# A hybrid RWKV-7 / attention block: inverse square roots as one GpSimd power, RWKV outputs transposed in squares of 32, removal products on GpSimd

## The chip, the cores and the metric

The kernel runs on one core of one Trainium2 chip. The metric is the device time of one execution in microseconds (us); lower is better. Five engines work side by side, each through its own queue in order: TensorE (PE, matrix products), VectorE (DVE), ScalarE (ACT), GpSimd (POOL) and SyncE (SP, which issues most of the loads). An instruction that needs another engine's result waits on a semaphore at the head of its queue, and everything behind it waits too.

## The reference

One layer on 256 tokens of width 2048, in fp32. Only the RWKV branch is touched in substance:

```python
u = rms_norm(h); z = u @ w_in                       # split into RWKV, attention and gate columns
kk = heads(k * k_k)                                 # 16 heads of 64
kk = kk / jnp.maximum(jnp.sqrt(jnp.sum(kk * kk, axis=-1, keepdims=True)), 1e-12)
k = k * (1 + (a - 1) * k_a)
# scan over tokens; -kk and kk * a are the removal ("delta rule") vectors
sa = einsum(state, -kk_t);  state = state * w_t + sa * (kk_t * a_t) + v_t * k_t;  y_t = einsum(state, r_t)
y = (y - mean) * lax.rsqrt(var + 64e-5)             # per head
y = y * lnx_w + lnx_b
y_rw = (y + bonus) * g
mix = (sigmoid(gA) * (y_rw @ Wa) + sigmoid(gB) * (y_mla @ Wb)) @ W_out
h += rms_norm(mix); h += rms_norm(gated MLP(h)); h += rms_norm(sigmoid(h @ W_pg) * (p @ W_ple))
```

There are inverse square roots in every `rms_norm`, in the normalization of `kk` and in the per-head normalization of `y`.

## The kernel before

All weights stream from HBM in chunks of 128x1024 fp32 (`wchunk`, L135). Each half of 512 columns is split into a rounded part `hi` (ACT cast, L148) and a rest `lo` (DVE subtraction, L149), five buffers each, so that a product in fp32 is made of three faster ones: hi by hi, hi by rest, lo by hi. `dense` and `fm3` (L183 to L185) do that with weights stationary, `fm` (L170, L174) and `tm` (L196 to L200) for the later layers. So each 512 columns of weights cost one ACT and one DVE instruction, all through the program.

The RWKV heads go in eight pairs (128 partitions: two heads of 64), two pairs at a time, which makes four duos. `rw_pair` (L714) is a generator: each `yield` names how many units of dense work (one unit is six matmuls of 128x256) are emitted before its next step. A loop at the end advances up to three duos together: `cur` runs the state recurrence, `nxt` prepares the next duo's operands, `old` finishes the former duo's outputs, and between the steps `work` emits the dense matmuls of the input, gate and attention-output projections. So PE's queue is dense matmuls with the duo's small matmuls strewn in; the tile framework then places the instructions of each engine by priority and by its own estimates of when they can start. Which instruction stands where in a queue is fixed when the program is built.

What the change and the prediction's steps touch:

- `rsqrt` (L206): an inverse square root on DVE without a table. A first guess from the bit pattern (L208), a first correction (L212 to L214, or L210 and L214 where there is one column) and a second one (L218 to L222, or L216 to L222). That is nine small instructions for 2 or 4 columns, seven for one column. `rstd_col` (L224) scales a sum of squares (L227) and calls it: three times near the start, after w_out and w_down and in between (two columns), and in `finish` (L1326), once for each half of the tokens, at the end (one column).
- In `rw_pair`, preparation: squares of `kk` are summed by PE (`pq`, L768), clamped (L771) and rooted into `nv`; ACT spreads the root (`rb`, L775), PE transposes it (`nr`, L779), DVE multiplies (`kk`, L781). Then `kr` (L786, L787), the removal products `be` = kk times a (L790) and its scaled form in `bk` (L791), and `a` is overwritten in place (L792). POOL copies part of `bk` (L797). PE uses `bk` and `kr` in `pg` (L818).
- In `rw_pair`, recurrence: four chunks of `pc` products on PE (L940, L944, L953) with short ACT and DVE steps between them (`R` L942, `av` L946, `sv` L955). Each waits for the one before.
- In `rw_pair`, tail: mean and variance of `y` (L970 to L977), `rsqrt` into `gs`, the multiplication (L982); eight matmuls of 64x64 a pair against the identity transpose `y` into PSUM (`pm`, L988), ACT evacuates with scale and bias (`yf`, L990), DVE adds the bonus (L992), PE makes the gate `pgt` (L995 to L998), DVE multiplies (L999), and the result is split into `yrw` (L161, L162), which the branch product (L1087 on) reads.
- POOL otherwise does memsets and copies (`vw` L830/L831, `kb` L825, `Xb` L900, `av` L930) and later six additions (L1090).

Of the kernel before, what the change touches and what calls it, by code (L numbers as in the profile page):

```python
# [108 lines left out]
def hybrid_block(tc, A):  # L109
# [50 lines left out]
    def split(hi, lo, src):  # L160
        act(hi, src, AF.Copy)  # L161
        tt(out=lo, in0=src, in1=hi.bitcast(F32), op=ALU.subtract)  # L162
# [39 lines left out]


    RA, RB = 1.681914091, 0.703952253

    def rsqrt(dst, v, w):  # L206
        t, p = w
        ts(out=dst.bitcast(I32), in0=v.bitcast(I32), scalar1=-0.5, scalar2=float(0x5F1FFFF9), op0=ALU.mult, op1=ALU.add)  # L208
# [12 lines left out]
        tt(out=p, in0=p, in1=t, op=ALU.mult)
        stt(out=dst, in0=p, scalar=-1.875 * RB, in1=dst, op0=ALU.add, op1=ALU.mult)  # L222
# [491 lines left out]
    def rw_pair(J, j, k, r, v):  # L714
        par = j % 2

        def e1(nm, shape=None, dt=F32):
# [52 lines left out]
        nv = sp.tile([P, 4, 4], F32, name="nv")  # L770
        ts(out=nv[:, 0, :], in0=pq[:, 0:4], scalar1=1e-24, scalar2=None, op0=ALU.max)  # L771
# [3 lines left out]
        act(rb[:], nv[:, 1, :].unsqueeze(2).to_broadcast([P, 4, C]), AF.Copy)  # L775
# [14 lines left out]
        tt(out=be[:], in0=kk[:], in1=a[:], op=ALU.mult)  # L790
        tt(out=bk[:, :, 0:C], in0=c4(be[:]), in1=c4(pin[:]), op=ALU.mult)  # L791
# [176 lines left out]
        gs = sp.tile([P, 5, NCH], F32, name="gs")  # L968
# [14 lines left out]
        yield NONE, STEP
        yield NONE, STEP
        pm = small("pm")
        for c in range(NCH):
            for hs in (lo_, hi_):
                mm(pm[hs, c * C:c * C + C], y[hs, c, :], ident[hs, hs], start=c == 0, stop=c == NCH - 1)  # L988
# [1 line left out]
        act(y[:], pm[:, 0:T], AF.Identity, scale=V("lnx_w", j), bias=V("lnx_b", j))  # L990
# [1 line left out]
        tt(out=y[:], in0=y[:], in1=bo[:], op=ALU.add)  # L992
# [453 lines left out]
```

## Time and profile before

| quantity | value |
|---|---|
| time, median of 3 runs | 1560.78 us (1560.56 to 1561.42) |
| the profiled execution's own time | 1560.39 us |
| its span in the trace | 1558.6 us |
| busy, PE / DVE / ACT / POOL | 1538.0 / 1182.2 / 942.1 / 60.9 us |
| instructions in the trace, PE / DVE / ACT / POOL | 10850 / 2670 / 1944 / 125 |
| mean granted TensorE clock | 0.997 |
| RWKV duos | from 180 us to 586 us in the span |

A row of a group gives line, engine, operation, output and inputs by the program's names, shape, count, then busy time, mean duration in ns and the idle time of the engine just before them. A row of the timeline gives start, duration, engine, line, operation, and in brackets how long the engine had idled and what released it; instructions of the same line that follow each other are merged with their count. Matmuls overlap in PE's pipeline, so the distance from start to start is what one costs, not its duration. DVE's small instructions overlap in the same way by some tens of ns.

### The profile page before, as it was taken

The page shows a single profiled execution, that of the slowest core. Times are in us where ns is not written, and L with a number is a line of the kernel's source. Part 1 is how long each engine was busy: PE and PEld are TensorE (multiplying, and loading weights), DVE is VectorE, ACT ScalarE, POOL GpSimd, SP SyncE. Part 2 cuts the span into 40 slices and gives each one's busy share as a digit, 9 for nine tenths or more (in the row PEclk, how much of TensorE's full clock was granted, in tenths as well). Part 3 has the DMA queues.
Part 4 walks back from the last instruction along what each step waited for, and adds up shares of the span by engine and source line. Part 5 has one row for each costly group of instructions (what it writes and reads, how often), then busy time and mean ns, then how long its engine had stood idle before and what let it go on. Part 6 is the DMA issues. An engine that isn't in the chain of part 4 may idle for free.

```text
span 1558.6 us, 29636 instructions
## 1 busy us (share of the span) xinstructions
PE 1538.0 (99%) x10850; PEld 1388.3 (89%) x10850; DVE 1182.2 (76%) x2670; ACT 942.1 (60%) x1944; POOL 60.9 (4%) x125
## 2 busy tenths in 40 slices
PE   9999999999999999999999999999999999999997
PEld 9989999999999999887888888888888888888886
DVE  7896687898989776557787777777777655777866
ACT  7686756566565555456766555555655555776653
POOL 0000201101011102000000000000000000000000
PEclk9999999999999999999999999999999999999998
DMA  8654555454444546865656555565655666666564
GB/s 304 192 172 141 154 173 164 138 171 129 147 150 136 160 153 200 306 199 167 203 174 205 198 181 202 179 203 179 206 181 190 175 192 195 197 197 191 166 200 148
DMA packets 80482, 285.19 MB, mean 183 GB/s; under 512 B 9040, under 2 KB 10320, under 8 KB 80336
## 3 DMA queue, kind: packets, MB, share of 16 engines
q1 hardware_dynamic: 77760, 279.48, 56.3%
q10 hardware_dynamic: 2576, 3.81, 0.7%
q8 instruction: 85, 1.39, 0.4%
q14 instruction: 61, 0.50, 0.1%
HBM read 281.16 MB, written 2.10 MB: 182 GB/s over the span
## 4 chain that ended last, share of the span: by engine, by line
PE 89%; DVE 6%; ACT 2%; DMA 1%; issue 1%; DVEq 0%; ACTq 0%
PE d L170 21%; PE d L174 11%; PE d L183 9%; PE d L185 8%; PE d L184 8%; PE o L196 7%; PE o L198 6%; PE o L200 6%; PE e L196 2%; PE e L198 2%; PE e L200 2%; DVE lo L149 2%; ACT hi L148 1%; DMA raw<-in_w_in 1%; PE tr L237 0%
## 5 line engine op out<-in xcount | busy, mean ns | idle before, releaser
L149 DVE TENSOR_TENSOR lo<-raw,hi 128x512 fp32r<-128x512 f32 x684 | 461.0, 690 | 213.9 <-ACT hi L148 208.5
L148 ACT CAST hi<-raw 128x512 fp32r<-128x512 f32 x684 | 410.7, 619 | 297.9 <-PE o L200 97.9
L183 PE MATMUL d<-uT,hi 128*128 128x256 f32 x1072 | 307.7, 287 | 0.7 <-ACT hi L161 0.6
L170 PE MATMUL d<-u,highs 128*128 128x512 f32 x1312 | 305.5, 390 | 0.0
L185 PE MATMUL d<-uT,lo 128*128 128x256 f32 x1072 | 300.5, 280 | 0.7 <-DVE lo L162 0.2
L184 PE MATMUL d<-uT,hi 128*128 128x256 f32 x1072 | 299.6, 279 | 0.1
L170 PEld LDWEIGHTS d<-u,highs 128*128 128x128 f32 x1312 | 243.3, 188 | 48.9
L148 ACT CAST highs<-raw 128x512 fp32r<-128x512 f32 x328 | 186.8, 616 | 115.0 <-DMA raw<-in_w_up 80.3
L183 PEld LDWEIGHTS d<-uT,hi 128*128 128x128 f32 x1072 | 201.7, 188 | 2.8 <-ACT hi L161 0.8
L185 PEld LDWEIGHTS d<-uT,lo 128*128 128x128 f32 x1072 | 201.5, 188 | 2.1 <-DVE lo L149 1.1
L184 PEld LDWEIGHTS d<-uT,hi 128*128 128x128 f32 x1072 | 201.7, 188 | 0.4 <-DVE uT L290 0.3
L149 DVE TENSOR_TENSOR hi<-raw,highs 128x512 fp32r<-128x512 f32 x164 | 112.7, 688 | 76.8 <-PE d L174 58.8
L174 PE MATMUL d<-u,lo 128*128 128x256 f32 x752 | 117.7, 280 | 0.0
L149 DVE TENSOR_TENSOR lo<-raw,highs 128x512 fp32r<-128x512 f32 x164 | 112.0, 684 | 0.0
L174 PE MATMUL d<-u,hi 128*128 128x256 f32 x656 | 103.3, 279 | 0.0
L174 PEld LDWEIGHTS d<-u,lo 128*128 128x128 f32 x752 | 101.7, 188 | 0.8
L174 PEld LDWEIGHTS d<-u,hi 128*128 128x128 f32 x656 | 91.5, 188 | 3.5
L198 PE MATMUL o<-lo,fsplit 128*128 128x512 f32 x264 | 88.6, 389 | 0.0
L196 PE MATMUL o<-hi,fsplit 128*128 128x512 f32 x264 | 88.5, 389 | 0.0
L200 PE MATMUL o<-hi,fsplit 128*128 128x512 f32 x264 | 88.4, 389 | 0.0
L1228 ACT ACTIVATE cy<-d 128x512 f32<-128x512 f32 x44 | 26.2, 597 | 67.8 <-PE d L174 67.8
L198 PEld LDWEIGHTS o<-lo,fsplit 128*128 128x128 f32 x264 | 49.6, 188 | 10.7 <-DVE lo L149 0.3
(389 smaller groups left out, 2550.9 us busy)
## 6 DMA issues: line engine op xcount, KB each, us to landing
raw<-in_w_up SPq DMA_DIRECT2D x176, 512.0 KB, 4.3
raw<-in_w_in SPq DMA_DIRECT2D x133, 512.0 KB, 3.6
raw<-in_w_down SPq DMA_DIRECT2D x88, 512.0 KB, 4.3
raw<-in_w_out SPq DMA_DIRECT2D x32, 512.0 KB, 4.4
raw<-in_w_pg SPq DMA_DIRECT2D x32, 512.0 KB, 3.6
raw<-in_w_bm SPq DMA_DIRECT2D x16, 512.0 KB, 3.7
raw<-in_w_br SPq DMA_DIRECT2D x16, 512.0 KB, 3.7
raw<-in_w_kv SPq DMA_DIRECT2D x8, 512.0 KB, 3.6
```

What stands on the lines that cost most here:

```text
L148: nc.scalar.copy(hi[:], raw[:, c:c + 512])
L149: tt(out=lo[:], in0=raw[:, c:c + 512], in1=hi[:].bitcast(F32), op=ALU.subtract)
L170: mm(ps[:, c, :], hi(i, col, P), mov[i][2], start=first and x == 0 and i == 0, stop=False)
L174: mm(ps[:, c, 0:T], lo(i, col, P), mov[i][0], start=False, stop=last and x == len(parts) - 1 and i == len(mov) - 1)
L183: mm(ps[:, c, :], hi(i, col, P), mov[i][:, 0:T], start=f, stop=False)
L184: mm(ps[:, c, :], hi(i, col, P), mov[i][:, T:2 * T], start=False, stop=False)
L185: mm(ps[:, c, :], lo(i, col, P), mov[i][:, 0:T], start=False, stop=l)
L196: mm(b[:], h, hi(i, g * 512, 512), start=f, stop=False)
L198: mm(b[:], h, lo(i, g * 512, 512), start=False, stop=False)
L200: mm(b[:], x, hi(i, g * 512, 512), start=False, stop=l)
L1228: act(y[:], ps[:, :, 0:T], AF.Copy)
```

## The change

1. `rsqrt` becomes one GpSimd `tensor_tensor` with the operation `pow`; the exponent -0.5 stands in eight columns of `st`. The clamp or the scaling ahead of it stays on DVE. In `rw_pair` the two pairs of a duo share one tile, and the second pair's step takes both pairs' eight columns in one power.
2. The tail's transposition: DVE transposes `y` in squares of 32x32 (one instruction a pair), ACT copies all of it, and four GpSimd copies a pair move the squares off the diagonal, across quadrants of 32 partitions. The eight `pm` matmuls are gone. Scale and bias, which ACT did at the evacuation, move into two DVE instructions that replace the two of L992 and L999. The tail has one `yield` less.
3. The removal products `be` and the part of `bk` made from it go from DVE to GpSimd. The in-place update of `a` stays on DVE, after them.

```diff
--- before.py
+++ after.py
@@ -200,32 +200,16 @@
                     mm(b[:], x, hi(i, g * 512, 512), start=False, stop=l)
 
 
-
-    RA, RB = 1.681914091, 0.703952253
-
-    def rsqrt(dst, v, w):
-        t, p = w
-        ts(out=dst.bitcast(I32), in0=v.bitcast(I32), scalar1=-0.5, scalar2=float(0x5F1FFFF9), op0=ALU.mult, op1=ALU.add)
-        if dst.shape[1] == 1:
-            ts(out=t, in0=dst, scalar1=dst, scalar2=v, op0=ALU.mult, op1=ALU.mult)
-        else:
-            tt(out=t, in0=dst, in1=dst, op=ALU.mult)
-            tt(out=t, in0=t, in1=v, op=ALU.mult)
-        stt(out=dst, in0=t, scalar=-RA / RB, in1=dst, op0=ALU.add, op1=ALU.mult)
-        if dst.shape[1] == 1:
-            ts(out=t, in0=dst, scalar1=dst, scalar2=v, op0=ALU.mult, op1=ALU.mult)
-        else:
-            tt(out=t, in0=dst, in1=dst, op=ALU.mult)
-            tt(out=t, in0=t, in1=v, op=ALU.mult)
-        ts(out=p, in0=t, scalar1=-0.375 * RB ** 5, scalar2=1.25 * RB ** 3, op0=ALU.mult, op1=ALU.add)
-        tt(out=p, in0=p, in1=t, op=ALU.mult)
-        stt(out=dst, in0=p, scalar=-1.875 * RB, in1=dst, op0=ALU.add, op1=ALU.mult)
+    nc.gpsimd.memset(st[:, 48:56], -0.5)
+
+    def rsqrt(dst, v):
+        nc.gpsimd.tensor_tensor(out=dst, in0=v, in1=st[:, 48:48 + dst.shape[1]], op=ALU.pow)
 
     def rstd_col(dst, ss, n):
-        v = sp.tile([P, 6], F32, name="rv")
+        v = sp.tile([P, 2], F32, name="rv")
         w = dst.shape[1]
         ts(out=v[:, 0:w], in0=ss, scalar1=1.0 / n, scalar2=1e-6, op0=ALU.mult, op1=ALU.add)
-        rsqrt(dst, v[:, 0:w], (v[:, 2:2 + w], v[:, 4:4 + w]))
+        rsqrt(dst, v[:, 0:w])
 
 
     def to_fm(ptile, dst, rows, gain, kbs):
@@ -767,12 +751,17 @@
         for t in range(2):
             mm(pq[:, 2 * t:2 * t + 2], sq[:, t * P:t * P + P], K("hsel", 0, 2), start=t == 0, stop=t == 1)
         yield NONE, STEP
-        nv = sp.tile([P, 4, 4], F32, name="nv")
-        ts(out=nv[:, 0, :], in0=pq[:, 0:4], scalar1=1e-24, scalar2=None, op0=ALU.max)
-        rsqrt(nv[:, 1, :], nv[:, 0, :], (nv[:, 2, :], nv[:, 3, :]))
+
+        if par == 0:
+            J["nv"] = sp.tile([P, 2, 2, 4], F32, name="nv")
+        nv = J["nv"]
+        ts(out=nv[:, 0, par, :], in0=pq[:, 0:4], scalar1=1e-24, scalar2=None, op0=ALU.max)
+        if par == 1:
+            nvs = [nv[:, i].rearrange("p r n -> p (r n)") for i in range(2)]
+            rsqrt(nvs[1], nvs[0])
         yield NONE, STEP
         rb = e1("rb", [P, 4, C])
-        act(rb[:], nv[:, 1, :].unsqueeze(2).to_broadcast([P, 4, C]), AF.Copy)
+        act(rb[:], nv[:, 1, par, :].unsqueeze(2).to_broadcast([P, 4, C]), AF.Copy)
         yield NONE, STEP
         nr = small("nr")
         for t in range(2):
@@ -787,8 +776,8 @@
         tt(out=kr[:, :, C:P], in0=c4(r), in1=pp[:, :, 1:C + 1], op=ALU.mult)
         yield NONE, STEP
         be = e1("be")
-        tt(out=be[:], in0=kk[:], in1=a[:], op=ALU.mult)
-        tt(out=bk[:, :, 0:C], in0=c4(be[:]), in1=c4(pin[:]), op=ALU.mult)
+        nc.gpsimd.tensor_tensor(out=be[:], in0=kk[:], in1=a[:], op=ALU.mult)
+        nc.gpsimd.tensor_tensor(out=bk[:, :, 0:C], in0=c4(be[:]), in1=c4(pin[:]), op=ALU.mult)
         ts(out=a[:], in0=a[:], scalar1=V("k_a", j), scalar2=oka[:, j:j + 1], op0=ALU.mult, op1=ALU.add)
         yield NONE, STEP
         kp = e1("kp")
@@ -965,7 +954,9 @@
         act(y[:], cc(py), AF.Copy)
         yield TAIL, STEP
 
-        gs = sp.tile([P, 5, NCH], F32, name="gs")
+        if par == 0:
+            J["gs"] = sp.tile([P, 3, 2, NCH], F32, name="gs")
+        gs = J["gs"][:, :, par]
         bc4 = lambda ap: ap.unsqueeze(2).to_broadcast([P, NCH, C])
         nc.vector.tensor_reduce(out=gs[:, 0, :], in_=y[:], axis=AX.X, op=ALU.add)
         ts(out=gs[:, 0, :], in0=gs[:, 0, :], scalar1=1.0 / C, scalar2=None, op0=ALU.mult)
@@ -976,28 +967,32 @@
         nc.vector.tensor_reduce(out=gs[:, 1, :], in_=sq[:], axis=AX.X, op=ALU.add)
         ts(out=gs[:, 1, :], in0=gs[:, 1, :], scalar1=1.0 / C, scalar2=64e-5, op0=ALU.mult, op1=ALU.add)
         yield NONE, STEP
-        rsqrt(gs[:, 2, :], gs[:, 1, :], (gs[:, 3, :], gs[:, 4, :]))
-        for _ in range(3):
-            yield NONE, STEP
+        if par == 1:
+            g8 = [J["gs"][:, i].rearrange("p r n -> p (r n)") for i in range(3)]
+            rsqrt(g8[2], g8[1])
+        yield NONE, STEP
+        yield NONE, STEP
         tt(out=y[:], in0=y[:], in1=bc4(gs[:, 2, :]), op=ALU.mult)
-        yield NONE, STEP
-        yield NONE, STEP
-        pm = small("pm")
-        for c in range(NCH):
-            for hs in (lo_, hi_):
-                mm(pm[hs, c * C:c * C + C], y[hs, c, :], ident[hs, hs], start=c == 0, stop=c == NCH - 1)
-        y = e1("yf")
-        act(y[:], pm[:, 0:T], AF.Identity, scale=V("lnx_w", j), bias=V("lnx_b", j))
-        yield NONE, STEP
-        tt(out=y[:], in0=y[:], in1=bo[:], op=ALU.add)
+
+        yt = e1("yt", [P, NCH, 2, 32])
+        nc.vector.transpose(out=yt[:].rearrange("p c b n -> p (c b n)"), in_=y[:].rearrange("p c n -> p (c n)"))
+        yield NONE, STEP
+        y = e1("yf", [P, NCH, 2, 32])
+        act(y[:], yt[:], AF.Copy)
+        for i in range(4):
+            nc.gpsimd.tensor_copy(y[Q[i ^ 1], :, i % 2, :], yt[Q[i], :, 1 - i % 2, :])
+        yield NONE, STEP
+        yield NONE, STEP
+        y = y[:].rearrange("p c b n -> p (c b n)")
+        stt(out=y, in0=y, scalar=V("lnx_w", j), in1=bo[:], op0=ALU.mult, op1=ALU.add)
         yield NONE, STEP
         pg = small("pgt")
         mm(pg[:, 0:T], lgs[:, 0, :], LM[:, 3, :], start=True, stop=False)
         mm(pg[:, 0:T], lgs[:, 0, :], LM[:, 4, :], start=False, stop=False)
         mm(pg[:, 0:T], lgs[:, 2, :], LM[:, 3, :], start=False, stop=False)
         mm(pg[:, 0:T], lgs[0:96, 1, :], LM[0:96, 5, :], start=False, stop=True)
-        tt(out=y[:], in0=y[:], in1=pg[:, 0:T], op=ALU.mult)
-        split(yrw[:, j, 0:T], yrw[:, j, T:2 * T], y[:])
+        stt(out=y, in0=y, scalar=V("lnx_b", j), in1=pg[:, 0:T], op0=ALU.add, op1=ALU.mult)
+        split(yrw[:, j, 0:T], yrw[:, j, T:2 * T], y)
 
     def gate(i, tag="zt"):
```

How the queues change, at three places. In the rows, `lo<-raw,hi` is the weight split of L149, and the brackets name the engines whose semaphores the instruction waits for.

DVE where the second duo's preparation and the first duo's recurrence meet, before (`kk` normalized, then the removal products, the update of `a`, and the recurrence's `sv`):

```order
L781 TENSOR_TENSOR kk<-kk,nr 128x256 [waits PE_49] x2
L786 TENSOR_TENSOR kr_4252<-kk,pp_3889 128x4x64 [waits DVE_49]
L786 TENSOR_TENSOR kr_4256<-kk,pp_3894 128x4x64 [waits DVE_49]
L149 TENSOR_TENSOR lo<-raw,hi 128x512 [waits PE_49,Activation_49]
L946 TENSOR_SCALAR av<-pc 64x64 [waits Activation_49] x2
L790 TENSOR_TENSOR be<-kk,a 128x256 x2
L149 TENSOR_TENSOR lo<-raw,hi 128x512 [waits DMAHW3_49,PE_49,Activation_49]
L791 TENSOR_TENSOR bk_4251<-be,pin 128x4x64 [waits DVE_49]
L792 TENSOR_SCALAR a<-a,vec,oka 128x256
L955 SCALAR_TENSOR_TENSOR sv<-pc,pp_2647,s_4170 64x64 [waits PE_49]
```

The same place on DVE after the change:

```order
L770 TENSOR_TENSOR kk<-kk,nr 128x256 [waits PE_49] x2
L775 TENSOR_TENSOR kr_4193<-kk,pp_3848 128x4x64 [waits DVE_49]
L775 TENSOR_TENSOR kr_4197<-kk,pp_3853 128x4x64 [waits DVE_49]
L149 TENSOR_TENSOR lo<-raw,hi 128x512 [waits PE_49,Activation_49]
L935 TENSOR_SCALAR av<-pc 64x64 [waits Activation_49] x2
L781 TENSOR_SCALAR a<-a,vec,oka 128x256 [waits Pool_49] x2
L149 TENSOR_TENSOR lo<-raw,hi 128x512 [waits DMAHW3_49,PE_49,Activation_49]
L784 TENSOR_TENSOR kp<-z_2469,a 128x256 [waits DVE_49] x2
L944 SCALAR_TENSOR_TENSOR sv<-pc,pp_2624,s_4111 64x64 [waits PE_49]
```

The products are gone, and both updates of `a` stand together behind a wait for POOL, ahead of the recurrence's `sv`.

DVE in the first duo's tail, before (the end of both pairs' chains for the root, then the multiplication of `y` by it; `gm` belongs to the second duo):

```order
L220 TENSOR_SCALAR gs<-gs 128x4 [waits DVE_49]
L219 TENSOR_TENSOR gs<-gs 128x4 [waits DVE_49]
L221 TENSOR_TENSOR gs<-gs 128x4 [waits DVE_49]
L220 TENSOR_SCALAR gs<-gs 128x4 [waits DVE_49]
L222 SCALAR_TENSOR_TENSOR gs<-gs 128x4 [waits DVE_49]
L221 TENSOR_TENSOR gs<-gs 128x4 [waits DVE_49]
L821 TENSOR_TENSOR gm_4521<-pg_4571,cst 128x8x64 [waits PE_49]
L222 SCALAR_TENSOR_TENSOR gs<-gs 128x4 [waits DVE_49]
L821 TENSOR_TENSOR gm_4521<-pg_4572,cst 128x8x64 [waits PE_49]
L982 TENSOR_TENSOR y<-y,gs 128x256
L982 TENSOR_TENSOR y<-y,gs 128x256 [waits DVE_49]
```

The same place after the change:

```order
L968 TENSOR_SCALAR gs<-gs 128x4 [waits DVE_49]
L967 TENSOR_REDUCE gs<-sq_4457 128x4 [waits Activation_49]
L149 TENSOR_TENSOR lo<-raw,hi 128x512 [waits DMAHW1_49,PE_49,Activation_49]
L968 TENSOR_SCALAR gs<-gs 128x4 [waits DVE_49]
L975 TENSOR_TENSOR y<-y,gs 128x256 [waits Pool_49]
L975 TENSOR_TENSOR y<-y,gs 128x256
L149 TENSOR_TENSOR lo<-raw,hi 128x512 [waits PE_49,Activation_49]
L810 TENSOR_TENSOR gm_4461<-pg_4494,cst 128x8x64 [waits PE_49]
```

The chains are gone, eighteen small instructions for the two pairs, and the multiplication stands directly behind the last scaling (L968), with a wait for POOL.

POOL from the third duo's recurrence to the fourth duo's preparation, before:

```order
L930 COPY av<-sv 128x512 [waits Activation_49]
L797 COPY bk_7228<-bk_7228 64x4x64 [waits DVE_49,Pool_49]
L797 COPY bk_7232<-bk_7232 64x4x64 [waits DVE_49]
L830 MEMSET vw 64x4x64 [waits PE_49]
L831 COPY vw<-z_4933 64x4x64
```

The same place after the change:

```order
L919 COPY av<-sv 128x512 [waits Activation_49]
L206 TENSOR_TENSOR nv<-nv,st 128x8 [waits DVE_49]
L779 TENSOR_TENSOR be<-kk,a 128x256 [waits DVE_49]
L780 TENSOR_TENSOR bk_7085<-be,pin 128x4x64 [waits Pool_49]
L779 TENSOR_TENSOR be<-kk,a 128x256 [waits DVE_49]
L786 COPY bk_7085<-bk_7085 64x4x64 [waits Pool_49]
L780 TENSOR_TENSOR bk_7089<-be,pin 128x4x64 [waits Pool_49]
L786 COPY bk_7089<-bk_7089 64x4x64 [waits Pool_49]
L819 MEMSET vw 64x4x64 [waits PE_49]
```

The power and the four products have come in; the second pair's `be` stands behind the first pair's `be` and `bk`.

More of the change, by code (lines that the diff above doesn't have):

```diff
@@ L978, in rw_pair @@
         yield NONE, STEP
-        rsqrt(gs[:, 2, :], gs[:, 1, :], (gs[:, 3, :], gs[:, 4, :]))
-        for _ in range(3):
-            yield NONE, STEP
-        tt(out=y[:], in0=y[:], in1=bc4(gs[:, 2, :]), op=ALU.mult)
+        if par == 1:
+            g8 = [J["gs"][:, i].rearrange("p r n -> p (r n)") for i in range(3)]
+            rsqrt(g8[2], g8[1])
         yield NONE, STEP
         yield NONE, STEP
-        pm = small("pm")
-        for c in range(NCH):
-            for hs in (lo_, hi_):
-                mm(pm[hs, c * C:c * C + C], y[hs, c, :], ident[hs, hs], start=c == 0, stop=c == NCH - 1)
-        y = e1("yf")
-        act(y[:], pm[:, 0:T], AF.Identity, scale=V("lnx_w", j), bias=V("lnx_b", j))
-        yield NONE, STEP
-        tt(out=y[:], in0=y[:], in1=bo[:], op=ALU.add)
+        tt(out=y[:], in0=y[:], in1=bc4(gs[:, 2, :]), op=ALU.mult)
+        yt = e1("yt", [P, NCH, 2, 32])
+        nc.vector.transpose(out=yt[:].rearrange("p c b n -> p (c b n)"), in_=y[:].rearrange("p c n -> p (c n)"))
+        yield NONE, STEP
+        y = e1("yf", [P, NCH, 2, 32])
[6 more added lines that the diff above has]
+        stt(out=y, in0=y, scalar=V("lnx_w", j), in1=bo[:], op0=ALU.mult, op1=ALU.add)
         yield NONE, STEP
```

## The prediction

> **What bounds the kernel now.** I read the page first: the busy shares of the engines and the chain of work that ended last. Then a table by stage, PE's waits, and the timeline at the places where the change cuts.
>
> ```profile
> PE 1538.0 (99%) x10850; PEld 1388.3 (89%) x10850; DVE 1182.2 (76%) x2670; ACT 942.1 (60%) x1944; POOL 60.9 (4%) x125
> PE 89%; DVE 6%; ACT 2%; DMA 1%; issue 1%; DVEq 0%; ACTq 0%
> 240.00:515.00 275.00, 271.01 (x3014) 263.35 (x3013) 238.57 (x762) 164.02 (x383) 33.83 (x76) 1.00 0.48 146
> 1549.00:1558.60 9.60, 0.00 (x0) 0.00 (x0) 5.84 (x16) 0.88 (x3) 0.00 (x0) 0.59 0.49 182
> PE pc L940 <- DVE sv L955: 1.9, 4, 0.9
> PE px L882 <- DVE YH L893: 1.7, 4, 0.6
> PE tr L237 <- DVE u L241: 0.8, 2, 0.6
> ```
>
> PE sets the time: busy 99% of the span, and 89% of the last chain. The third row is the middle of the RWKV duos (the columns after the length are PE, PEld, DVE, ACT, POOL): of 275 us PE idles 4.0, while DVE is busy 87%, against 76% over the whole span. The three waits show what the idling is: PE stands for DVE in the recurrence, a few tenths at a time. So a matmul removed in this stage is worth nearly its whole issue distance, and DVE work removed there is worth at most a part of those 4.0 us. The fourth row is the end: PE has nothing left in the last 9.6 us, and what stands there in a chain counts in full. POOL is idle 96% of the time.
>
> **The `pm` matmuls go.** The group of all of them, one duo's as the timeline shows them, and the next dense matmul:
>
> ```profile
> L988 PE MATMUL pm<-cst,y 64*64 64x64 f32 x128 | 4.6, 221 | 0.0
> 316.98 1.15 PE L988 MATMUL pm<-cst,y 64*64 64x64 f32 x32
> 318.06 0.38 PE L183 MATMUL d<-uT,hi 128*128 128x256 f32 x1
> ```
>
> PE is occupied from 316.98 to 318.06, 1.08 us a duo, and 4 duos make **4.3 us** (the group's 4.6 counts the modelled ends). The matmuls around them are dense work that was ready, so that time comes back: -4.3. What replaces them lies on DVE, ACT and POOL, and its result is read by PE at the end of the stage only (below).
>
> **The roots leave DVE.** In `rw_pair` a root is nine instructions like the first row below, twice a pair; the other rows are what else DVE loses or gets.
>
> ```profile
> L222 DVE SCALAR_TENSOR_TENSOR gs<-gs 128x4 f32<-128x4 f32 x8 | 1.3, 158 | 0.0
> L790 DVE TENSOR_TENSOR be<-kk,a 128x256 f32<-128x256 f32 x8 | 3.0, 417 | 0.1
> L791 DVE TENSOR_TENSOR bk<-be,pin 128x256 f32<-128x256 f32 x8 | 3.4, 421 | 0.2
> L992 DVE TENSOR_TENSOR yf<-yf,bo 128x256 f32<-128x256 f32 x8 | 3.3, 417 | 0.3 <-ACT yf L990 0.3
> L888 DVE STREAM_TRANSPOSE YH<-Xc 128x128 f32<-128x128 f32 x8 | 2.2, 295 | 0.0
> L800 DVE SCALAR_TENSOR_TENSOR rk<-z,vec,kp 128x256 f32<-128x256 f32 x8 | 4.0, 494 | 0.0
> ```
>
> Removed: 16 x 9 x 0.158 = 22.8 us of roots and 8 x (0.417 + 0.421) = 6.7 us of products. Added: eight transposes of 256 columns, at most twice the 0.295 of 128, so 4.7 us, and 16 x (0.494 - 0.417) = 1.2 us because the two instructions behind them become three-operand ones like L800. Net DVE is relieved of about 23.6 us in a stage where PE's waits come from it. Bounds of what that is worth: nothing, if the recurrence's own latency makes the waits, and 2.5 us, if the waits for `sv` and `YH` fall by two thirds. I take **-1.0**, a quarter of the 4.0 idle, since the removed instructions stand beside only some of the waits.
>
> **What the power costs in `rw_pair`.** No row shows a power on POOL. The nearest ones:
>
> ```profile
> L754 POOL MEMSET pp<- 128x4 f32 x8 | 0.7, 112 | 0.3
> L1090 POOL TENSOR_TENSOR g<-g,mix 128x512 f32<-128x512 f32 x6 | 9.6, 1604 | 69.3 <-ACT hi L148 48.7 <-DVE g L1089 20.6
> 272.41 0.16 DVE L771 TENSOR_SCALAR nv<-pq 128x4 f32<-128x4 f32 x1 [0.96 <-PE pq L768]
> 273.82 0.16 DVE L771 TENSOR_SCALAR nv<-pq 128x4 f32<-128x4 f32 x1
> 277.62 0.42 ACT L775 ACTIVATE rb<-nv 128x256 f32<-128x256 f32 x1 [0.38 <-DVE nv L222]
> 279.71 0.60 PE L779 MATMUL nr<-cst,rb 128*128 128x128 f32 x4
> 308.58 0.16 DVE L977 TENSOR_SCALAR gs<-gs 128x4 f32<-128x4 f32 x1
> 311.42 0.15 DVE L222 SCALAR_TENSOR_TENSOR gs<-gs 128x4 f32<-128x4 f32 x1
> 284.90 0.42 DVE L791 TENSOR_TENSOR bk<-be,pin 128x256 f32<-128x256 f32 x1
> 285.45 0.46 POOL L797 COPY bk<-bk 64x256 f32<-64x256 f32 x1 [15.88 <-DVE bk L791]
> ```
>
> The lower end is a small POOL instruction without arithmetic, 0.11 us; the upper end 1.60, the dearest POOL instruction here, 512 columns of a product against the power's eight. I take 1.0: nine passes of the smallest kind, as many as the DVE chain had. [...]
>
> The way from DVE to POOL is 0.13 us (285.32 to 285.45). For `nv` both clamps are done at 273.98, the power at 275.1, where the chain ended near 277.6; PE reads the spread roots at 279.71, behind two ACT steps of 0.42. So the new chain has 278.87 - 274.11 = **4.8 us** before PE waits, and costs nothing at 1.0. For `gs` the scaling ends at 308.74 and the old chain at 311.57, 2.8 us; now DVE itself stands at the multiplication of `y` for 0.13 + 1.0, with the weight splits and the second duo's `gm` behind it, but in a place where 2.8 us of its own chain stood. No cost; the cover is the removed chain, and beyond it the five buffers of `lo`.
>
> **The removal products on POOL.** The added wait is DVE's: both `a` updates wait for the second `be`, which stands in POOL's queue behind the first pair's `be` and `bk`. Behind `a` stand a weight split, `kp` and the recurrence's `sv`, for which PE waits already.
>
> ```profile
> 281.17 0.75 DVE L781 TENSOR_TENSOR kk<-kk,nr 128x256 f32<-128x256 f32 x2
> 282.51 0.68 DVE L149 TENSOR_TENSOR lo<-raw,hi 128x512 fp32r<-128x512 f32 x1
> 285.24 0.41 DVE L792 TENSOR_SCALAR a<-a,vec,oka 128x256 f32<-128x256 f32 x1
> 286.58 0.90 DVE L955 SCALAR_TENSOR_TENSOR sv<-pc,pp,s 64x64 f32<-64x64 f32 x3
> 595.54 0.68 DVE L149 TENSOR_TENSOR lo<-raw,hi 128x512 fp32r<-128x512 f32 x1
> 595.70 1.68 POOL L1090 TENSOR_TENSOR g<-g,mix 128x512 f32<-128x512 f32 x1 [4.81 <-DVE g L1089]
> L797 POOL COPY bk<-bk 64x256 f32<-64x256 f32 x8 | 6.7, 840 | 70.1 <-DVE bk L791 70.1
> ```
>
> The first `kk` is there at 281.59, POOL starts at 281.72. Half of L1090's 1604 ns is 0.80 a product: three end at 284.1, two updates at 284.9, the split 285.6, both `kp` (0.75) 286.3, four `sv` (1.2) 287.5. Before, `sv` ended at 287.48. Even, then. But POOL's time stretches beside DVE: the same copy took 0.46 in the timeline and 0.84 on average. At that ratio of 1.8 a product takes 1.46 and `sv` comes 2.0 us later. The range is 0 to 2.0 in each of three duos (the first has no recurrence beside it); I take 0.3 each, **+0.9**, near the low end, because the last rows show a POOL product with DVE beside it at 1.68.
>
> [...] The row at 595.70 does not show a full block: the product started inside DVE's split, which ran until 596.22, and took 1.68 against 1.60, not 0.5 more. [...]
>
> **The moved squares.** Eight copies a duo like `Xb`:
>
> ```profile
> L900 POOL COPY Xb<-Xc 32x128 f32<-32x128 f32 x32 | 13.1, 408 | 180.7 <-DVE Xc L897 179.4
> 582.59 0.28 PE L183 MATMUL d<-yrw,hi 128*128 128x256 f32 x1
> 585.36 0.42 DVE L162 TENSOR_TENSOR yrw<-yf,yrw 128x256 fp32r<-128x256 f32 x1
> 587.54 0.28 PE L183 MATMUL d<-yrw,hi 128*128 128x256 f32 x1
> ```
>
> Those are 3.3 us of POOL a duo (a shift across quadrants is taken to cost what `Xb`'s in-place quadrants cost). In the first three duos nobody but DVE's two closing instructions waits, two yields later. In the last duo PE reads the eight blocks of `yrw` from 582.59 on, 0.7 us each, the last one at 587.54, 1.8 us after its split ended (585.78). The tail loses 1.1 us of `pm`, a yield and 1.7 us of root chain (2.8 against 1.13), and gains 3.3 of copies and some 0.5 of transposes: about 1 us later at most, so covered. If copies took 0.84, it would cost 2.6 once.
>
> **The other roots.** Near the start and after w_out and w_down the chain has dense matmuls beside it; PE's rows give 0.8 us of waits there in all (`tr`), and I take nothing, between -0.7 and +0.7. The end is different:
>
> ```profile
> 1551.05 0.15 DVE L208 TENSOR_SCALAR st<-rv 128x1 int32<-128x1 int32 x1
> 1552.62 2.08 DVE L1334 SCALAR_TENSOR_TENSOR h<-e,st,h 128x512 f32<-128x512 f32 x3
> ```
>
> Seven instructions from 1551.05 to 1552.62, 1.57 us, become 0.13 + power + some 0.05 back. With the power at 0.9 for one column the gain is **-0.5**; by the ends 0.11 and 1.60 it is -1.3 to +0.2.
>
> **Sum.** -4.3 - 1.0 + 0.9 - 0.5 = -4.9 against the profiled execution's own 1560.39 (span 1558.6 and 1.8 around it): 1555.5. The median of the runs lies 0.4 above that execution, so I forecast **1555.9** for it. About 0.2%, 3.1 us, is what a measurement of this kernel can tell from no change, so faster means under 1557.7 and slower over 1563.9.
>
> **The rivals.** First, slower: the power is dear per column. From 4.8 us for eight columns on, each further us holds PE at `nr` in every duo; the other terms save 1.2 a duo, so the change loses from about 6 us a power, 0.75 a column. At 1 us a column PE stands 3.2 us in each of four duos, +13 - 4.9 = +8, 1569; at 2 us a column 45 of waits, about 1601, and `gs` adds DVE's standing. For: no row prices a power. Against: 512 columns of a product cost 1.60, 3 ns a column. Chance 0.15.
>
> [...] Chance 0.16. [...]
>
> Third, the freed PE time does not come back, because the recurrence's latency paces the stage: only the end's -0.5 and the products' +0.9 are left, 1561.2. For: PE waits for `sv` four times. Against: 271 of 275 us busy. Chance 0.07.
>
> **The numbers.** My case has 0.62, with a range of its own from -4.3 - 2.5 - 1.3 = -8.1 (1552.7) to -4.3 + 0.9 + 0.2 = -3.2 (1557.6; no relief, the dearer end). With the second and third rival the range holds 0.85, so it goes from **1552.5 to 1562.0** (1561.2 and the 0.6 by which the slowest run before lay over its median), and leaves the first out. Faster 0.62 and 0.04 of the second rival's better side, 0.66; same 0.12 + 0.07 = 0.19; slower 0.15.
>
> **What would show it.** Right: PE's busy time in the duos falls by about 4; the power of eight columns at or under 1.6 us; DVE under 82% in 240 to 515; no PE wait at `nr`; the root at the end under 1.57. Wrong: a power over 4.8 us; PE rows that wait for `sv` or `kk` more than now, with DVE idle at `a` behind POOL; `be` over 1.2 us; or PE idle in the stage grown by what `pm` gave.

## The result and the profile after

The changed kernel takes 1570.17 us (median of 6 runs, 1566.54 to 1571.79), the kernel before 1560.94 beside it: a ratio of 1.0051, 95% interval 1.0034 to 1.0068. By the ratio it is slower by some 8 us (the medians lie 9.2 apart), where I forecast 1555.9. Of the profile after, first the two rows that answer to the busy times and the stage of the prediction's first fence, in the same columns.

```profile
PE 1540.1 (98%) x10722; PEld 1390.1 (89%) x10722; DVE 1164.2 (74%) x2450; ACT 939.4 (60%) x1944; POOL 105.6 (7%) x190
...
240.00:515.00 275.00, 265.00 (x2871) 256.48 (x2871) 224.86 (x619) 158.52 (x378) 64.90 (x118) 0.99 0.47 143
```

DVE is relieved in the duos as forecast (82% of the 275 us), yet PE idles 10.0 us there in place of 4.0. PE's waits from 235 to 760 us name whom it waits for:

```profile
PE ph L871 <- DVE YH L877: 4.3, 2, 2.3
PE pc L942 <- DVE av L935: 2.3, 2, 1.5
PE pc L929 <- DVE sv L944: 2.2, 4, 1.2
PE d L183 <- ACT hi L148: 1.6, 1, 1.6
PE d L185 <- DVE lo L149: 0.9, 1, 0.9
```

Before, PE never stood for `ph` (the first matmuls of the block inversion), for `av` in `pc`, or for `hi`. To see what each wait is worth I took each matmul's start in the two traces, paired them in order, and read how late the same matmul is. This table, called the ledger below, has that lateness in us, at marks in the time of the kernel before, counted from 240; a difference between two marks is called a step:

```
mark      300   325   360   400   415   450   490   510   575   586   612   745  1480
after    +1.4  +0.1  +4.4  +4.9  +3.6  +4.8  +6.7  +5.4  +5.4  +4.1  +9.7 +10.1 +10.4
```

Four steps of -1.3 (300 to 325, 400 to 415, 490 to 510, 575 to 586) are the `pm` matmuls that are gone, 5.2 in all. Against them stand: +1.4, +0.5 and +1.9 (to 300, 400 and 490) in the recurrences beside which GpSimd forms the products; +4.3 and +1.2 (325 to 360, 415 to 450) at two inversions; **+5.6 behind the last duo** (586 to 612); +0.4 and +0.3 at the roots of rows after w_out and w_down. The end of the kernel gives 0.8 back (last matmul to end of span 9.4 us, 10.1 before), and 0.5 lies outside the table (0.3 ahead of 240, 0.2 behind 1530); together that is the 10.1 us by which the span grew. I take the places one by one.

**The products.** First GpSimd's and then VectorE's timeline at the second duo's products:

```profile
282.13 0.74 POOL L779 TENSOR_TENSOR be<-kk,a 128x256 f32<-128x256 f32 x1 [6.30 <-DVE kk L770]
282.95 0.80 POOL L780 TENSOR_TENSOR bk<-be,pin 128x256 f32<-128x256 f32 x1
283.70 0.92 POOL L779 TENSOR_TENSOR be<-kk,a 128x256 f32<-128x256 f32 x1
```

```profile
282.30 1.73 DVE L775 TENSOR_TENSOR kr<-kk,pp 128x256 f32<-128x256 f32 x2
283.95 1.22 DVE L149 TENSOR_TENSOR lo<-raw,hi 128x512 fp32r<-128x512 f32 x1
...
285.61 1.25 DVE L781 TENSOR_SCALAR a<-a,vec,oka 128x256 f32<-128x256 f32 x2
```

The `kr` pair takes 1.73 and the split 1.22 (0.69 elsewhere), each beside a product that had started before it. The groups of 240 to 515, before and after:

```profile
L786 DVE TENSOR_TENSOR kr<-kk,pp 128x256 f32<-128x256 f32 x6 | 2.3, 418 | 0.0
L792 DVE TENSOR_SCALAR a<-a,vec,oka 128x256 f32<-128x256 f32 x6 | 2.4, 408 | 0.0
```

```profile
L775 DVE TENSOR_TENSOR kr<-kk,pp 128x256 f32<-128x256 f32 x6 | 5.2, 901 | 0.0
L781 DVE TENSOR_SCALAR a<-a,vec,oka 128x256 f32<-128x256 f32 x6 | 3.8, 670 | 0.1
```

`kr` more than doubles, 0.42 to 0.90, and the `a` update goes from 0.41 to 0.67. `sv` and `av`, queued behind them, come late.

**The inversion.** GpSimd's powers are short, as the first fence has them (groups of the whole kernel), but VectorE stands at each of the four behind the recurrence. Its waits from 240 to 600 are next, then its timeline around the first of them, with PE's row at the inversion:

```profile
L206 POOL TENSOR_TENSOR gs<-gs,st 128x8 f32<-128x8 f32 x4 | 7.7, 1924 | 45.0 <-DVE gs L968 45.0
L206 POOL TENSOR_TENSOR nv<-nv,st 128x8 f32<-128x8 f32 x4 | 6.6, 1638 | 14.9 <-DVE nv L758 14.9
```

```profile
DVE y L975 <- POOL gs L206: 6.4, 4, 1.8
...
DVE yf L987 <- POOL yf L983: 1.7, 3, 1.0
```

```profile
312.22 0.76 DVE L975 TENSOR_TENSOR y<-y,gs 128x256 f32<-128x256 f32 x2 [1.82 <-POOL gs L206]
313.50 2.48 DVE L810 TENSOR_TENSOR gm<-pg,cst 128x512 f32<-128x512 f32 x4
...
346.36 0.50 DVE L877 STREAM_TRANSPOSE YH<-Xc 128x128 f32<-128x128 f32 x2
346.72 0.75 PE L871 MATMUL ph<-YH,n 32*32 32x32 f32 x64 [2.29 <-DVE YH L877]
```

In the kernel before, the same places read so:

```profile
310.82 0.68 DVE L821 TENSOR_TENSOR gm<-pg,cst 128x512 f32<-128x512 f32 x1
312.09 0.75 DVE L982 TENSOR_TENSOR y<-y,gs 128x256 f32<-128x256 f32 x2
...
341.55 0.50 DVE L888 STREAM_TRANSPOSE YH<-Xc 128x128 f32<-128x128 f32 x2
342.85 0.75 PE L882 MATMUL ph<-YH,n 32*32 32x32 f32 x64
```

Before, the root's instructions and two of the next duo's `gm` filled DVE up to the multiplication of `y`. Now DVE stands 1.82 us at it, with all four `gm` behind; the two transposes (0.72) follow; and by a count in the two traces 202 weight splits are done when `YH` comes, in place of 200. From the first sum over `y` to `YH` DVE takes 42.3 us (304.05 to 346.36) in place of 39.3 (302.26 to 341.55). PE comes to `ph` with 1.3 us of `pm` less on its way and stands 2.29. Then its clock falls to half for 3.4 us (348.2 to 351.6). The step of +4.3 has three parts: 1.2 us are lost from 330 to 340, where PE takes up weights only as their split on DVE ends (at 333.53 behind the one that ends at 333.47), 2.3 are the stall, and 0.8 come behind it. The table of stretches shows the clock, here and behind the last duo (last columns: granted clock, DMA share, GB/s):

```profile
344.00:347.00 3.00, 0.71 (x36) 0.51 (x35) 2.93 (x10) 0.93 (x3) 0.00 (x0) 1.00 0.46 167
348.00:351.00 3.00, 3.00 (x20) 2.78 (x22) 2.39 (x7) 1.54 (x4) 0.00 (x0) 0.53 0.74 255
598.00:602.00 4.00, 1.48 (x8) 1.08 (x8) 2.49 (x4) 1.66 (x3) 1.07 (x1) 0.85 0.36 147
602.00:607.00 5.00, 5.00 (x26) 5.00 (x25) 4.17 (x6) 2.18 (x4) 1.73 (x2) 0.50 0.55 128
```

**Behind the last duo.** ACT's rows of the kernel before and of the changed one:

```profile
584.62 0.41 ACT L161 ACTIVATE yrw<-yf 128x256 fp32r<-128x256 f32 x1
585.81 0.41 ACTq L1077 DMA_DIRECT2D e<-in_pT  x1
591.26 0.63 ACT L161 ACTIVATE pS<-e 128x512 fp32r<-128x512 f32 x1 [2.30 <-DMA e<-in_pT]
```

```profile
590.41 0.42 ACT L161 ACTIVATE yrw<-yf 128x256 fp32r<-128x256 f32 x1 [0.57 <-DVE yf L994]
591.32 0.42 ACTq L1072 DMA_DIRECT2D e<-in_pT  x1
598.84 0.63 ACT L161 ACTIVATE pS<-e 128x512 fp32r<-128x512 f32 x1 [5.86 <-DMA e<-in_pT]
```

The load of `pT` goes to memory that the RWKV stage frees with its last split, so it is issued 5.5 us later, 4.1 of which is the lateness of everything by then; it takes 7.5 us where it took 5.4. ACT stands for it 5.9 us with the `hi` of the next weights queued behind, and PE runs dry for 2.5 us (the rows for `hi` and `lo` in PE's waits). Then its clock is at half for 6.8 us (600.8 to 607.6). PE is busy for 6.15 of them, and half of that, 3.1, is lost: with the 2.5 that makes the 5.6.

### The profile page after: what moved, and what is told of

The parts are those of the page before. It is cut to its first block, busy times and chain, and to the rows that moved or that the text cites. A ratio compares the mean times of both kernels' runs of the same rounds, so it can differ in the third digit from the quotient of the medians.

```text
span 1568.7 us, 29262 instructions
## 1 busy us (share of the span) xinstructions
PE 1540.1 (98%) x10722; PEld 1390.1 (89%) x10722; DVE 1164.2 (74%) x2450; ACT 939.4 (60%) x1944; POOL 105.6 (7%) x190
## 4 chain that ended last, share of the span: by engine, by line
PE 81%; issue 8%; DVE 7%; ACT 2%; DMA 2%; POOL 0%; DVEq 0%; POOLq 0%; SPq 0%; ACTq 0%
PE d L170 20%; PE d L174 10%; PE d L183 8%; PE d L185 8%; PE d L184 8%; PE o L198 5%; PE o L196 5%; PE o L200 5%; DVE lo L149 3%; PE e L198 2%; PE e L196 2%; PE e L200 2%; ACT hi L148 1%; PE pg L807 1%; PE tr L221 0%
## 5 line engine op out<-in xcount | busy, mean ns | idle before, releaser
L149 DVE TENSOR_TENSOR lo<-raw,hi 128x512 fp32r<-128x512 f32 x684 | 463.3, 693 | 222.3 <-ACT hi L148 209.9
L149 DVE TENSOR_TENSOR hi<-raw,highs 128x512 fp32r<-128x512 f32 x164 | 112.8, 689 | 78.9 <-PE d L174 59.2
L149 DVE TENSOR_TENSOR lo<-raw,highs 128x512 fp32r<-128x512 f32 x164 | 112.1, 685 | 0.0
L206 POOL TENSOR_TENSOR st<-rv,st 128x2 f32<-128x2 f32 (+1 forms) x6 | 3.9, 655 | 875.7 <-DVE rv L211 875.7
```

The costliest lines, as they stand in the source:

```text
L149: tt(out=lo[:], in0=raw[:, c:c + 512], in1=hi[:].bitcast(F32), op=ALU.subtract)
```

## The experiments

**Theory A**: the loss is three late chains: the products slow DVE beside them; DVE's queue ahead of the inversion grows (wait for the root, transposes, splits) and PE stands there; `pT` comes late. Its rivals are named in the expectations. Each experiment gives the median time, then the ratio to the kernel before on the same chip, with its 95% interval. "Undone" means that part of the change's diff reversed, "alone" that part put into the kernel before.

**1. `pT` in a buffer of its own**, in the changed kernel:

```diff
-    ep = es_e.enter_context(tc.tile_pool(name="ep", bufs=1))
+    ep = ...; pfp = cp.tile([P, 2, T], F32, name="pf")
...
-    pf = e[:, 0, 0:2 * T].rearrange("p (k t) -> p k t", k=2)
+    pf = pfp[:]
```

> The changed kernel, with pT loaded at the start into a buffer of its own (2 KB a partition more) instead of into memory that the RWKV stage has to free first. Nothing else moves but the step that reads it. Theory A (three late chains: the products that slow DVE beside them, the wait for the roots with the inversion behind it, and the load of pT that is queued behind the last rows of yrw): the stall at 598 us of the changed kernel, 5.4 us with the slower clock behind it, goes, and 1570.2 becomes about 1564.8, 1.0025 of the kernel before. Rival B (PE stands there because the last yrw rows are late, not for pT): PE still stands 2 us or more before 600 and the time stays within 1 us of 1570.

It took 1564.65 us, 1.0023 (1.0014 to 1.0031). PE's waits no longer hold the rows for `hi` and `lo`, and ACT's row is

```profile
592.71 0.63 ACT L161 ACTIVATE pS<-pf 128x512 fp32r<-128x512 f32 x1
```

Lateness goes from +5.4 at 586 to +5.2 at 612, where it rose by 5.6. The `yrw` rows came no earlier than in the changed kernel, so rival B falls.

**2 to 4. One part undone each.**

```diff
# u_products
-        nc.gpsimd.tensor_tensor(out=be[:], in0=kk[:], in1=a[:], op=ALU.mult)
-        nc.gpsimd.tensor_tensor(out=bk[:, :, 0:C], ...)
+        tt(out=be[:], in0=kk[:], in1=a[:], op=ALU.mult)
+        tt(out=bk[:, :, 0:C], ...)
# u_pairroots: nv and gs by the nine VectorE instructions of the kernel before
# u_squares: pm matmuls and ACT's read of them in place of transposes and copies
```

> The changed kernel with the two removal products (be and the first third of bk) back on VectorE; roots and squares as changed. Theory A: kr falls from 0.90 to 0.42 us and the a update from 0.67 to 0.41, PE's steps for sv and av (1.4 + 0.5 + 1.7 us over three duos) go, and the inversion's stall at 340 us shrinks by the 1.4 us that it inherited: 4 to 6 us back, 1564 to 1566. Rival C (contention of VectorE and GpSimd is the whole loss, the late chains follow from it): also the stalls at 340 and 598 go, 1556 to 1558. Rival D (the roots are the loss): 1569 to 1570.

It took 1565.55 us, 1.0030 (1.0020 to 1.0041). `kr` is back at its old time, with no step at 300, 400 or 490 (lateness +0.2, +1.8, +1.4 against +1.4, +4.9, +6.7):

```profile
L775 DVE TENSOR_TENSOR kr<-kk,pp 128x256 f32<-128x256 f32 x6 | 2.3, 418 | 0.0
```

The inversions still hold PE 4.3 us and `pT` still costs 4.1, so contention is not the whole loss: theory A. The stall at the first inversion did not shrink by 1.4 as theory A had it; its step is +2.8 in place of +4.3 because the clock did not fall behind it here: PE gains 0.6 there, where it lost 0.8 in the changed kernel.

> The changed kernel with the two roots of each pair (nv and gs) back on VectorE as nine instructions each; the roots of rows stay powers on GpSimd, products and squares as changed. VectorE gets 22.8 us of work back and loses the wait for gs (6.4 us over four duos). Theory A: the inversion of the second duo comes about 1 us earlier, sv stays late, so 0 to 3 us back, 1567 to 1570. Rival D (the wait of VectorE for the power, with both pairs merged, is the loss): the stalls at 340, 435 and 598 go, 1557 to 1560.

It took 1569.35 us, 1.0050 (1.0038 to 1.0062): hardly better. DVE no longer waits for the power but does the root itself, and PE stands at `ph` for the same 4.3 us. Rival D falls.

> The changed kernel with the pm matmuls back in place of the 32-squares (ACT reads them with gain and bias as before); roots and products as changed. PE gets 5.1 us of matmuls back (1.28 a duo by the ledger of the two traces). Theory A: the yrw rows of the last duo come some 2 us earlier, which is less than the 2.5 us that PE stood for pT but enough to avoid the slower clock, and the second inversion's stall shrinks by the two transposes (0.9 us): 1567 to 1571. Rival E (the squares with their GpSimd copies are the loss): stalls at 340 and 598 both go, 1562 to 1564.

It took 1566.75 us, 1.0033 (1.0021 to 1.0045), just under theory A's range. With `pm` back the waits are

```profile
PE pc L942 <- DVE av L935: 2.3, 2, 1.5
PE pc L929 <- DVE sv L944: 2.1, 4, 1.2
PE px L871 <- DVE YH L882: 1.4, 3, 0.5
```

The row for `ph` is gone, and so is the step at `pT` (+5.5 at 586 and at 612), more of it than I expected. No half clock is left in the trace but at its start and its very end. Here rival E said more of the mechanism than I did: it is the squares that hold PE at the inversion and behind the last duo. It was wrong on the time, as the products' and rows' steps stay.

**5 to 8. One part alone, and `pm` merely left out.** `no_pm` leaves the transposition out and puts nothing in its place.

```diff
# no_pm, in the kernel before
-                mm(pm[hs, c * C:c * C + C], y[hs, c, :], ident[hs, hs], ...)
-        y = e1("yf")
+                pass
+        y, pm = e1("yf"), y[:].rearrange("p c n -> p (c n)")
```

> The kernel before with the 128 pm matmuls left out: ACT applies gain and bias to y as it lies, so the heads stay untransposed (that part of the computation is left out). Nothing takes their place. Theory A (PE time freed ahead of a wait that VectorE's inversion ends comes back only where no such wait follows): 1.3 us each in the last two duos, and part of it at most in the two duos behind which PE waits for the inversion: 1557 to 1559. Rival, the step of my forecast (the dense work behind it was ready, so all of it comes back): 1560.9 - 4.3 to 5.1, 1555.8 to 1556.6.

It took 1556.11 us, 0.9963 (0.9950 to 0.9975). All of it comes back, 5.2 us at mark 700: here theory A was wrong and the forecast's step right. PE waits 1.5 us for `ph`, and catches up behind it.

> The kernel before with the squares alone: transposes on VectorE, half of them moved by ACT and half by GpSimd, the two closing three-operand instructions; roots and products stay on VectorE. Theory A: -1.3 us a duo from PE, but VectorE has some 1 us more a duo ahead of the inversion, so PE waits 2 us more at the inversions of the second and third duo, and pT comes some 1.5 us late once: 1559 to 1562. Rival, my forecast's terms for this edit (-4.3 for pm, covered copies, some of the added VectorE work felt): 1556 to 1557.

It took 1566.35 us, 1.0028 (1.0017 to 1.0040), 10 us above `no_pm` and above both expectations. Its waits and clock:

```profile
PE ph L881 <- DVE YH L887: 4.3, 2, 2.3
...
344.00:348.00 4.00, 2.91 (x73) 2.85 (x74) 4.00 (x12) 2.44 (x6) 0.00 (x0) 0.58 0.57 164
348.00:352.00 4.00, 4.00 (x80) 3.71 (x80) 1.74 (x6) 0.62 (x1) 0.61 (x3) 0.57 0.52 154
440.00:444.00 4.00, 3.80 (x89) 3.60 (x92) 3.12 (x8) 1.78 (x5) 0.00 (x0) 0.57 0.66 225
```

From `y` to `YH` it takes 42.0 us, with 202 splits done: the squares alone make the inversion late. I had left out the half clock behind each stall, 6.8 us long from 344.6 and 3.4 us from 440.2, which adds up to 3.2 and 1.7 us (half of PE's busy time in it): lateness goes from -1.4 to +3.6 over the first inversion.

> The kernel before with the removal products alone on GpSimd. Theory A: kr takes 0.9 us and the a update 0.67 beside them, PE's steps for sv and av are there as in the changed kernel (1.4 + 0.5 + 1.7 us), and nothing else: 1564 to 1565.5. [...]

It took 1564.77 us, 1.0016 (1.0007 to 1.0025), with a lateness of +1.5, +2.0 and +4.0 at 300, 400 and 490, then flat. By the interval 1.1 to 3.9 us, by the ledger 3.9: theory A, and the squares are not needed for it.

> The kernel before with the roots alone as powers on GpSimd, those of rows and those of pairs. Theory A: the powers of rows cost PE some 0.5 us each at the two places behind w_out and w_down and give 0.3 back at the end; those of pairs give VectorE 2.2 us a duo and take 1.6 of waiting, so they are worth 0 to -1: 1560.5 to 1562. Rival D (the wait for the power is the loss): over 1565.

It took 1564.06 us, 1.0017 (1.0008 to 1.0026), some 2.7 us, more than theory A had. The steps are +0.9 at the powers of the second duo's `nv`, +1.5 ahead of the first inversion, where PE waits 0.6 for a split, +0.6 at the next, +0.5 and +0.3 at the roots of rows; no relief of DVE shows as a gain anywhere.

**9 to 12. Combinations without the products and with the roots of rows on VectorE.**

```diff
# best_y2: squares, pair roots on GpSimd, pT as in 1
# best_pmul: and
-        tt(out=y[:], in0=y[:], in1=bc4(gs[:, 2, :]), op=ALU.mult)
+        nc.gpsimd.tensor_tensor(out=y[:], in0=y[:], in1=bc4(gs[:, 2, :]), op=ALU.mult)
# hp_pmul: and, around pd, xc, Xc and the first YH
+                with tc.high_priority():
# hp_sq: squares, pT and priority, without the pair roots and without best_pmul's line
```

> Squares and pair roots as changed; products and the roots of rows back on VectorE; pT loaded early into its own buffer. Theory A, adding the steps of the ledgers so far: the four duos end 1.3 us ahead of the kernel before (four times 1.3 for pm, less two stalls of 2.2 us before the inversion, partly caught up), nothing is lost at 598, nor at the roots of rows: 1559.6, between 1558.5 and 1562 by whether the clock drops behind the two stalls. If the parts hinder each other in some other way: over 1562.

It took 1562.05 us, 1.0007 (0.9998 to 1.0016): 2 us above the sum, at the end of the range, and the ledger names why: 0.9 at the first duo's `nv`, where PE waits 0.7 for `rb`, and half clock behind both inversions.

> best_y2 with the multiplication of y by the root on GpSimd, behind the power, so that VectorE neither waits for the power (1.4 to 1.8 us) nor multiplies (0.75 us a duo). Theory A (VectorE's queue ahead of the inversion sets the stall): the inversions come 2 us earlier, the stalls at 340 and 435 fall to 0.5 us or less, and the time to 1556 to 1558. Rival C (what GpSimd takes over comes back as contention): gm, dm or splits beside the two products take up to 0.5 us more each, and the stalls stay over 1.2: 1559 to 1561.

It took 1559.47 us, 0.9991 (0.9982 to 1.0000): 2.6 us better by the medians, less than expected and in the range of rival C. From `y` to `YH` it takes 40.4 us in place of 42.3; but PE's stalls fell only from 4.3 to 3.7, with half clock behind both. The multiplications take GpSimd 0.61 us each, and no slowed DVE instruction shows beside them, so rival C's cause is not there. But the stall did not fall to 0.5 as theory A had it. As the inversion comes earlier so does PE, which no longer loses the 1.1 us that it lost ahead of the stall in `best_y2`, waiting for splits.

> best_pmul with the inversion's steps on VectorE given priority, by which one weight split fewer stands ahead of it in each duo. Theory A: the inversion comes 0.7 us earlier than in best_pmul; 0 to 1 us faster than that, 1556 to 1557.5. Rival: the split that is put behind it holds PE instead, and it is the same or slower than best_pmul.

It took 1558.52 us, 0.9979 (0.9969 to 0.9989), a little above the range. There are 201 splits ahead of `YH` and 39.5 us from `y` to it, and PE's two stalls are down to 2.2 in all, with no half clock behind them.

> The squares alone, as in a_squares, with pT loaded early and the inversion's steps given priority; all roots and products on VectorE. Theory A: against a_squares the pT step (2.1 us) goes, and the inversion comes 0.7 us earlier, so the stalls at 343 and 439 shrink to about 1.6 us and the clock drops less often: 1560 to 1562.5. Rival (priority or pT do nothing): 1564 or more.

It took 1560.94 us, 0.9996 (0.9987 to 1.0005): as theory A has it, with 41.2 us to `YH` and 2.5 of stall.

**13 and 14. What the gain comes from.**

```diff
# before_hp: pT and priority alone, in the kernel before
# hp_pmul_nv: hp_pmul with nv's root on VectorE, per pair
```

> The kernel before with two edits that hp_pmul has beside the change's: pT loaded early into its own buffer, and priority for the inversion's steps on VectorE. Theory A: before, PE waits 0.7 us in all for the inversion and none for pT, so there is little to gain: 1560 to 1561.5, and the gain of hp_pmul (2.7 us) is that of the squares once they don't delay the inversion. Rival (the gain is the priority's, not the squares'): 1558 to 1559.

It took 1561.08 us, 1.0002 (0.9993 to 1.0011): nothing, so the gain of the combinations is not that of the priority alone. Beside the squares it was worth 0.9 us by the medians (`best_pmul` to `hp_pmul`).

> hp_pmul with the root for nv back on VectorE per pair; only the root behind the recurrence and the multiplication by it stay on GpSimd. In hp_pmul PE waits 0.5 us at nr in the first duo, which goes; VectorE has 5 us more in all beside the recurrence, where it has idle time. Theory A: the stalls before the inversion stay as they are, the two steps at 199 and 257 us (0.7 and 0.4) shrink: 1557 to 1558.5. Rival (relief of VectorE is worth something anywhere): 1559 to 1560.5.

It took **1556.57 us, 0.9972 (0.9961 to 0.9983)**, a little under theory A's range: faster than both kernels, though GpSimd does less than in `hp_pmul`. DVE's and GpSimd's timelines at the root behind the recurrence:

```profile
309.73 2.48 DVE L825 TENSOR_TENSOR gm<-pg,cst 128x512 f32<-128x512 f32 x4
...
312.46 0.44 DVE L996 STREAM_TRANSPOSE yt<-y 128x256 f32<-128x256 f32 x1
```

```profile
308.74 1.66 POOL L206 TENSOR_TENSOR gs<-gs,st 128x8 f32<-128x8 f32 x1 [5.05 <-DVE gs L986]
310.47 1.19 POOL L993 TENSOR_TENSOR y<-y,gs 128x256 f32<-128x256 f32 x2
```

PE's largest wait for `ph` is now this row:

```profile
PE ph L888 <- DVE YH L895: 2.1, 2, 1.1
```

DVE goes straight on to `gm` and has done all four 10.0 us after the first sum over `y` (302.18), in the changed kernel 11.9 us after it, while GpSimd does root and multiplication. `YH` follows `y` after 39.5 us, nearly as in the kernel before; PE stands 2.1 us in all for `ph` with no half clock, and keeps 4.8 of the 5.2 us of `pm`.

## Why the prediction was wrong, step by step

- **The `pm` matmuls, -4.3: right**, a little small. Steps of 1.3 us a duo, 5.2 in all; `no_pm` returned them whole, so the third rival (freed PE time does not come back) falls too.
- **The step that failed: the squares' cover.** "In the first three duos nobody but DVE's two closing instructions waits." I asked who reads the result, and not what stands behind the transposes and closing instructions in DVE's queue: the next duo's shuffles and inversion, for which PE stands. DVE is busy 39.0 of the 42.3 us from `y` to `YH`, and 1.8 of the rest is its wait for the root, so each instruction put ahead of the inversion moves it. `a_squares` cost 4.4 us where these terms had -4.3, and undoing the squares cleared the stalls at the inversion and behind the last duo.
- **The same in the last duo: "covered".** I checked PE's reading of the last `yrw` block (1.8 us of slack) and overlooked the load of `pT`, which waits on ACT's queue for that split, with the `hi` of the weights behind it. The step was +5.6 us (2.5 dry, 3.1 by half clock), all gone in `pt_own`.
- **The wait for `gs`, "no cost": wrong.** "A place where 2.8 us of its own chain stood" took the chain's length for DVE's time. The chain's gaps had been filled with splits and `gm`; a wait in the queue fills with nothing. It came to 6.4 us over four duos. `u_pairroots` shows that this alone, with the squares in, hardly changed the time; without the squares, `a_roots` has steps of +1.5 and +0.6 at and ahead of the inversions; `best_pmul`, which ends the wait and moves the multiplication, gained.
- **DVE's relief, -1.0: worth nothing.** Over the kernel DVE's busy time fell 18.0 us (1182.2 to 1164.2) in place of 23.6; the rest is about what `kr` (8 x 0.48) and `a` (8 x 0.26) lengthened. `hp_pmul_nv` takes nv's relief back and is no slower.
- **The products, +0.9: mis-sized**, 2.5 by `a_products`' ratio and 3.8 by the steps. My second rival had GpSimd's `be` start only behind DVE's `kr` and split, by my estimate 1.5 us late in each of three duos, 4.6 in all; no run shows that wait. What the changed kernel's trace shows there is the other order: in these three duos the first `be` starts 0.17 us ahead of `kr` and takes 0.74 us, the second takes 0.92, and `kr` takes 0.90 in place of 0.42 and the split behind it 1.22 in place of 0.69. In the first duo, where each `be` starts inside a split (202.08 and 204.64), it takes 1.06 and 1.26. That the rival's 1.5 us a duo lies near the steps (1.4, 0.5, 1.9) is in part luck. I had read one row, at 595.70, as showing no full block: 1.68 against the group's 1.60. But all six products of that group start inside a split of DVE (the first at 589.36, in the split from 589.05), so 1.60 was no undisturbed time, and the row could tell nothing of a block.
- **The power, 1.0 us taken: 1.64 and 1.92**, just past the upper bound of 1.60, but far from the 6 at which the first rival decides; there is no PE wait at `nr` in the changed kernel. Slower was right, by another mechanism than that rival's.
- **The other roots, 0 within 0.7:** they measured +0.4 and +0.3. **The end, -0.5:** it measured -0.8, in range; the power of one column took 0.56 where seven instructions took 1.57. The upper end of the range adds up to 1561.8, not 1562.0; nothing hangs on it.

What stays open: why one split more stands ahead of the first inversion when `pm` goes (201 in `no_pm`) and two more with the squares (202); the order is the scheduler's. What a stall costs beyond its length is in part chance, by where it lies among the clock's stretches (last section). So the steps of a single trace at 360 and 612 hold up to 3.1 us each that another execution need not have.

## What to carry to other kernels

When a step moves to another engine, list what is queued behind every instruction that now waits or is added, not only who reads its result: here a wait of 1.8 us and 0.7 us of transposes made the next duo's inversion late, and PE stood for that. Move a chain whole: root and multiplication together on GpSimd freed VectorE, the root alone made it wait (6.4 us over four duos). And a load that reuses a stage's memory inherits that stage's lateness; a buffer of its own was worth 4.4 us here by the ratios and 5.5 by the medians.

## What the runs showed of the hardware

- PE's clock fell to half for 3.4 or 6.8 us behind some stalls of 1.8 to 2.5 us, so a stall cost up to some twice its length: 0.53 in 348 to 351 behind 2.3 us, 0.50 in 602 to 607 behind 2.5. Others of like length left it at 1.00 (the changed kernel at 440, `u_products` at 343 and 435). The traces of this case show what parts them here. In each of the seven with half clock between 60 and 1535 us its changes lie whole multiples of 3.41 us behind the trace's first clock record and so from each other. In the changed kernel that record is at 10.26 us and the changes lie at 348.18, 351.59, 600.77 and 607.59 (the granted clock is 0.59 in 348 to 349, 0.70 in 351 to 352, 0.88 in 600 to 601 and 0.70 in 607 to 608), which is 99 times 3.41 behind it, then 1, 73 and 2 times; in `a_squares` at 344.6, 351.4, 440.2 and 443.6, which is 2, 26 and 1 times. Cut into stretches of 3.41 us at these marks, from 60 to 1535 us, half clock followed all twelve stretches at full clock in which PE idled 1.79 us or more, one of the five with 1.68 to 1.76 (`u_products`, 593.2), and none of those with 1.66 or less: in these traces the limit lies near half a stretch. The stall at 440 in the changed kernel falls on a mark, which leaves 1.61 us in one stretch. At half clock one stretch with PE busy throughout brought the full clock back (the changed kernel, 348.2 to 351.6); with 0.5 to 0.7 us of idling it took a second (the changed kernel from 600.8, `a_squares` from 344.6).
- GpSimd's power took 1.64 to 1.92 us on average for eight columns in the changed kernel, 0.71 to 0.89 for two and 0.55 for one: by these rows an estimated 0.16 to 0.20 us a column on a base of some 0.4.
- VectorE's update of `a` took 0.67 us on average beside GpSimd's products in the changed kernel and 0.41 in the kernel before (240 to 515 us). The multiplication of `y` on GpSimd, with a broadcast operand, took 0.61 us on average in `best_pmul`.
